# Alternating 128-slot and 64-slot experts in a mixture-of-experts stage, with some down weights multiplied unsplit in fp32

## The chip, the cores and the metric

The kernel runs on one core of a Trainium2 chip. The metric is the device time of one execution, in microseconds (us). Engines are written as the profile writes them: PE is TensorE (PEld its weight loads), DVE is VectorE, ACT is ScalarE, POOL is GpSimd, SP is the queue that issues the weight transfers.

## What is computed

A network of three blocks on 256 tokens of width 1024, all in fp32. The change touches the mixture-of-experts layer of the second block:

```python
def moe_swiglu(h, w_router, w_gate_up, w_down):
    t = h.reshape(-1, D)                       # 256 x 1024
    logits = (t @ w_router).astype(F32)
    top_val, top_idx = lax.top_k(logits, 2)    # 8 experts, 2 for each token
    top_w = jax.nn.softmax(top_val, axis=-1)
    ...
    for e in range(8):
        gt, up = jnp.split(t @ w_gate_up[e], 2, axis=-1)   # 1024 x 7168
        y = (jax.nn.silu(gt) * up) @ w_down[e]              # 3584 x 1024
        out = out + combine[:, e:e + 1] * y
```

## The kernel before

**Split products.** [...] To keep fp32 precision each fp32 operand is split into a high part H (ACT copies it to fp32r) and a low part L (DVE subtracts H from the raw value). A product is then H·H + H·L + L·H: three matmuls (`mm3`, L219 to L221). The weight split is `split` at L215: an ACTIVATE `wH<-raw` and a TENSOR_TENSOR `wL<-raw,wH` for each tile of 128x2048 (1 MiB).

**The weight stream.** `stream` (L149) hands out weight tiles in order: SP loads a raw tile (L161), ACT and DVE split it, and the tile is given to PE after `ahead` = 2 further tiles have been asked for. In this stage raw tiles have 10 buffers (`more_weights`: 4 of a pool "more", the 5 of "wraw", 1 spare), H has 3 and L has 3. An expert has 28 tiles of gate and up weights (W1) and 14 of down weights (W2, two for each 512-row chunk j = 0 to 6).

**Experts.** `route` sorts the experts by their number of tokens (expert 0 is put first always). Turns 0 to 3 get 128 slots each, turns 4 to 7 get 64 slots. `gather` picks the tokens of a group of turns with one-hot matmuls (`oh`) and writes them to the one pair of buffers `hH`, `hL`. For a big turn x is (H, L) of 128 slots and each weight slice of 512 columns takes 3 matmuls. For a small turn H and L of the 64 slots lie side by side as one stationary operand of 128 columns: `product` (L1197) makes one matmul x·wH of 128 columns (L1207) and one of the first 64 columns with wL (L1210), so 2 matmuls. The two halves of the result are added later: for the gate by a matmul with the fp32 matrix `fold` (L1251; operands `fold` and `halves` are plain fp32), for the activations by DVE (`both`, L1295), after which `both` is split into the two halves of `aH`.

**Order.** The loop goes over turns and over steps of 512-column chunks js = (0,), (1, 2), (3, 4), (5, 6). `up` does W1 of a step, then `down` does W2 of the step before; `finish` splits the result (`yH`, `yL`) and `scatter` adds it to the residual `xs` (L1383). Groups of turns gathered together are

```python
        groups = ((0,), (1, 2), (3,), (4, 5, 6, 7))
```

A gather stands ahead of the turn that begins a group, in the last step of the turn before. A branch for experts that overflow their slots stands behind the loop.

Of the kernel before, what the change touches and what calls it, by code (L numbers as in the profile page):

```python
# [10 lines left out]
F32 = mybir.dt.float32  # L11
# [20 lines left out]
BIG_TURNS = 4  # L32
# [54 lines left out]
class Net:  # L87
# [836 lines left out]
    def route(self, f, sb, psum):  # L924
# [9 lines left out]
        nc.gpsimd.tensor_copy(ones, self.cst["ones"])  # L934
        ident = self.cst["ident"]
# [77 lines left out]
        def order(counts):  # L1013
# [13 lines left out]
            turn = small("turn", [NE])  # L1027
            nc.vector.tensor_reduce(turn, a, axis=AX.X, op=OP.add)
            iota = self.cst["iota"][:, :NE]
            nc.vector.tensor_tensor(p, turn[:, None, :].to_broadcast(shape), iota[:, :, None].to_broadcast(shape),  # L1030
# [15 lines left out]
            nc.vector.tensor_scalar(full[:, BIG_TURNS:], full[:, BIG_TURNS:], 64.0, None, op0=OP.add)  # L1046
# [12 lines left out]
    def gather(self, sb, psum, route, turns, iota):  # L1059

        nc = self.nc
        n, small = len(turns), turns[0] >= BIG_TURNS
        w = 64 if small else 128
        place = route["place"][:, :, turns[0]:turns[0] + n]
        oh = sb.tile([128, 2, 4 if small else 2, 128], F32R, name="oh")[:, :, :n]
        for t in range(2):
            shape = [128, n, 128 // w, w]  # L1070
            nc.vector.tensor_tensor(oh[:, t].rearrange("p e (d s) -> p e d s", s=w),
                                    iota[:, None, None, :w].to_broadcast(shape),
                                    place[:, t, :, None, None].to_broadcast(shape), op=OP.is_equal)
        H, L = self.h_parts(other=False)
        g, hp = self.cols["moe_norm"], route["hp"]
        cols = n * w
        per = 512 // cols
        for c0 in range(0, KC, per):
            ps = psum.tile([128, 512], F32, name="tp", tag="tp")
            for k in range(c0, c0 + per):  # L1080
                o = ps[:, (k - c0) * cols:(k - c0 + 1) * cols].rearrange("p (e s) -> p e s", s=w)
# [3 lines left out]
                if small:  # L1085
                    for x, d in ((H, slice(0, 2)), (L, slice(2, 4))):
                        v = x[:, k].rearrange("p (e h s) -> p e h s", e=2, h=2)
                        nc.scalar.activation(v[:, :, 0], o[:, d], AF.Copy, scale=g[:, k:k + 1])
                        nc.vector.scalar_tensor_tensor(v[:, :, 1], o[:, d], g[:, k:k + 1], v[:, :, 0].bitcast(F32),
                                                       op0=OP.mult, op1=OP.subtract)  # L1090
                else:
                    o = ps[:, (k - c0) * cols:(k - c0 + 1) * cols]
                    nc.scalar.activation(H[:, k, :cols], o, AF.Copy, scale=g[:, k:k + 1])  # L1093
                    nc.vector.scalar_tensor_tensor(L[:, k, :cols], o, g[:, k:k + 1], H[:, k, :cols].bitcast(F32),
                                                   op0=OP.mult, op1=OP.subtract)
        x = []
        for i in range(n):
            s = slice(i % 2 * 128, i % 2 * 128 + 128)
            x.append(((H, L)[i // 2][:, :, s],) if small else (H[:, :, s], L[:, :, s]))

        def factors():
            rs = sb.tile([128, 4], F32, name="r_slot", bufs=2)
            ps = psum.tile([128, 512], F32, name="r_ps", tag="tp")
            for i in range(2 * n):
                nc.tensor.matmul(ps[:, i // 2 * 2:i // 2 * 2 + 2], oh[:, i % 2, i // 2], route["r"][:, i % 2],
                                 start=i % 2 == 0, stop=i % 2 == 1)
            nc.vector.tensor_reduce(rs[:, :n], ps[:, :2 * n].rearrange("p (e i) -> p e i", i=2), axis=AX.X, op=OP.add)
            return rs

        return x, oh, factors  # L1110

    def experts(self, sb, psum, route, iota_big, iota_small, ahead, x=None):
# [50 lines left out]
        def put_off(n, f):  # L1163
            later.append([n, f])
# [10 lines left out]
        def ohT(e):  # L1175

            if e not in ohTs:
                oh, i0 = by["oh"], e - by["e0"]
                n = min(2, by["n"] - i0)
                t_ = sb.tile([128, 2, T], F32R, name="ohT")  # L1180
                ps = psum.tile([128, 512], F32, name="tp", tag="tp")
                for i in range(2 * n):
                    self.transpose(ps[:, i * 128:(i + 1) * 128], oh[:, i % 2, i0 + i // 2].bitcast(F32))
                nc.scalar.copy(t_[:, :n].rearrange("p e t -> p (e t)"), ps[:, :n * T])
                for i in range(n):
                    ohTs[e + i] = t_[:, i]
            return ohTs[e]

        def fetch(group):
            e = group[0]  # L1190
            by["x"], by["oh"], by["factors"] = self.gather(sb, psum, route, group, iota_small if e >= BIG_TURNS else iota_big)
            by["e0"], by["n"] = e, len(group)
# [41 lines left out]
        def up(e, js):  # L1234

            small = e >= BIG_TURNS
            w = 64 if small else 128
# [4 lines left out]
            xe, i0 = by["x"][e - by["e0"]], e - by["e0"]  # L1242
# [17 lines left out]
            if js[0] == 0 and i0 == 0:  # L1260
                by["r"] = by["factors"]()
            r = by["r"][:, i0:i0 + 1]
            oh = by["oh"]
            acts = []

            def activations():
                for g in range(len(js)):
# [3 lines left out]
                    if gates:  # L1271
                        for i in range(4):
                            mm(gate, oh[:, i // 2, 0], gates[i // 2][i % 2].rearrange("p c s -> p (c s)"), start=i == 0, stop=i == 3)
# [7 lines left out]
            def parts(g):  # L1281
# [6 lines left out]
                with behind():  # L1288
                    if small:
# [11 lines left out]
                made.setdefault((e, js[g]), []).extend(y)  # L1301
# [3 lines left out]
        def down(e, j):  # L1305
# [491 lines left out]
```

## Time and profile before

| | us |
|---|---|
| median of 3 runs (1814.49 to 1816.99) | 1814.55 |
| the profiled execution, its device time | 1817.69 |
| its span in the trace | 1815.9 |
| PE busy / DVE busy / ACT busy in the span | 1706.0 / 1453.5 / 1208.2 |

Device time stands 1.8 us above the span in the profiled execution. A row of the windows lists, after the length, the busy time of PE, PEld, DVE, ACT and POOL with instruction counts, the granted TensorE clock as a share of full speed, and the share and rate of the DMA engines. The expert loop takes about half of the span; the profile's shares of busy time are means over stages with different limits, so the loop is read from its own windows.

### The profile page before, as it was taken

Reading aid. Unit: us, or ns where it says so; the run is one execution under the profiler, and the core shown is the slowest. Engines: PE = TensorE matmul, PEld = TensorE weight load, DVE = VectorE, ACT = ScalarE, POOL = GpSimd, SP = SyncE. Lnnn points to the kernel's source line nnn. Section 1 sums busy time; section 2 is a strip of 40 time slices with the busy share of each in tenths; the row PEclk is TensorE's granted clock in tenths of the full one; section 3 lists DMA queues with packets and bytes.
Section 4 is the critical chain, followed back from the end, with each engine's and each line's share of the span. In section 5 each row is a group of like instructions: output and inputs, shape, how many; then the busy total and the mean of one; then the engine's idle time right before and its main releaser. Section 6 shows DMA issues by size and latency. Waiting matters only on the chain. (4 is left out here: it accounts for less than half of the span.)

```text
span 1815.9 us, 21998 instructions
## 1 busy us (share of the span) xinstructions
PE 1706.0 (94%) x7875; PEld 1304.0 (72%) x7875; DVE 1453.5 (80%) x1545; ACT 1208.2 (67%) x1490; POOL 79.3 (4%) x116
## 2 busy tenths in 40 slices
PE   8999999999999999999999988888888869989997
PEld 6767787788778888888888755555555547778886
DVE  4767888666769988898898999999999966575555
ACT  6665444576557777777777888887888855654443
POOL 2102000020100000000000000000000010000001
PEclk9999999999999999999999999999999979999999
DMA  8537999553458999999999999999999934355551
GB/s 273 163 97 276 341 340 322 180 167 117 146 203 298 404 362 370 358 355 360 354 338 359 351 378 403 402 404 408 401 404 401 366 129 152 127 173 182 177 178 43
DMA packets 175894, 511.29 MB, mean 282 GB/s; under 512 B 10293, under 2 KB 36021, under 8 KB 172576
## 3 DMA queue, kind: packets, MB, share of 16 engines
q1 hardware_dynamic: 172720, 501.84, 75.4%
q0 software_dynamic: 2608, 7.11, 1.5%
q8 instruction: 64, 1.05, 0.2%
q10 hardware_dynamic: 448, 0.86, 0.1%
q14 instruction: 54, 0.44, 0.1%
HBM read 508.68 MB, written 2.66 MB: 282 GB/s over the span
## 5 line engine op out<-in xcount | busy, mean ns | idle before, releaser
L215 DVE TENSOR_TENSOR wL<-raw,wH 128x2048 fp32r<-128x2048 f32 (+2 forms) x665 | 1047.0, 1604 | 222.7 <-issue 87.9
L215 ACT ACTIVATE wH<-raw 128x2048 fp32r<-128x2048 f32 (+2 forms) x665 | 886.4, 1364 | 313.8 <-PE gu L221 120.1
L220 PE MATMUL gu<-wL,hH 128*128 128x512 f32 x744 | 292.6, 394 | 0.1
L221 PE MATMUL gu<-wH,hL 128*128 128x512 f32 x744 | 291.7, 393 | 0.0
L219 PE MATMUL gu<-wH,hH 128*128 128x512 f32 x744 | 286.5, 395 | 2.2 <-ACT hH L1093 2.2
L221 PE MATMUL acc<-wH,aL 128*128 128x512 f32 x440 | 174.7, 397 | 0.0
L220 PE MATMUL acc<-wL,aH 128*128 128x512 f32 x440 | 174.2, 396 | 0.3 <-DVE wL L215 0.3
L219 PE MATMUL acc<-wH,aH 128*128 128x512 f32 x440 | 172.5, 403 | 0.0
L220 PEld LDWEIGHTS gu<-wL,hH 128*128 128x128 f32 x744 | 141.0, 190 | 31.4 <-DVE wL L215 1.6
L219 PEld LDWEIGHTS gu<-wH,hH 128*128 128x128 f32 x744 | 140.8, 190 | 31.6 <-ACT hH L1093 2.3
L221 PEld LDWEIGHTS gu<-wH,hL 128*128 128x128 f32 x744 | 140.5, 189 | 29.3 <-DVE hL L1726 0.4
L219 PE MATMUL mm<-wH,hH 128*128 128x512 f32 (+1 forms) x384 | 152.0, 396 | 0.8 <-ACT hH L1725 0.5
L220 PE MATMUL mm<-wL,hH 128*128 128x512 f32 (+1 forms) x384 | 150.2, 392 | 0.0
L221 PE MATMUL mm<-wH,hL 128*128 128x512 f32 (+1 forms) x384 | 149.4, 390 | 0.0
L1210 PE MATMUL gu<-wL,hL 128*64 128x512 f32 x224 | 88.7, 413 | 20.0 <-DVE wL L215 19.5
L1210 PE MATMUL acc<-wL,aH 128*64 128x512 f32 x224 | 91.9, 417 | 16.0 <-DVE wL L215 11.9
L1210 PE MATMUL gu<-wL,hH 128*64 128x512 f32 x224 | 88.6, 413 | 17.4 <-DVE wL L215 16.9
L221 PEld LDWEIGHTS acc<-wH,aL 128*128 128x128 f32 x440 | 82.6, 188 | 19.6 <-issue 0.6
L220 PEld LDWEIGHTS acc<-wL,aH 128*128 128x128 f32 x440 | 82.7, 188 | 19.0 <-DVE wL L215 1.3
L219 PEld LDWEIGHTS acc<-wH,aH 128*128 128x128 f32 x440 | 82.5, 188 | 17.5
L1207 PE MATMUL acc<-wH,aH 128*128 128x512 f32 x224 | 89.3, 402 | 1.7 <-DVE aH L215 1.7
L1207 PE MATMUL gu<-wH,hH 128*128 128x512 f32 x224 | 85.6, 396 | 0.5 <-ACT wH L215 0.5
(480 smaller groups left out, 2100.0 us busy)
## 6 DMA issues: line engine op xcount, KB each, us to landing
raw<-in_moe_w_gate_up_dram SPq DMA_DIRECT2D x224, 1024.0 KB, 7.1
raw<-in_moe_w_down_dram SPq DMA_DIRECT2D x112, 1024.0 KB, 7.7
raw<-in_w_ff_dram SPq DMA_DIRECT2D x32, 1024.0 KB, 5.2
raw<-in_w_ada_dram SPq DMA_DIRECT2D x24, 1024.0 KB, 5.6
raw<-in_dense_w_gate_up_dram SPq DMA_DIRECT2D x44, 512.0 KB, 5.7
raw<-in_b_w_in_dram SPq DMA_DIRECT2D x12, 1024.0 KB, 5.2
raw<-in_w_in_dram SPq DMA_DIRECT2D x12, 1024.0 KB, 5.1
raw<-in_dense_w_down_dram SPq DMA_DIRECT2D x11, 1024.0 KB, 5.2
```

The lines of the kernel that those rows point to most:

```text
L215: return self.nc.scalar.activation(H, src, AF.Copy), self.nc.vector.tensor_tensor(L, src, H.bitcast(F32), op=OP.subtract)
L219: mm(ps, xH, wH, start=start, stop=False)
L220: mm(ps, xH, wL, start=False, stop=False)
L221: mm(ps, xL, wH, start=False, stop=stop)
L1207: high = lambda: mm(ps, x[0], H, start=start, stop=stop)
L1210: mm(ps[:64], x[0][:, :64], L, start=False, stop=False)
```

## The change

Three edits. (1) The rank of the expert at each turn comes from `RANKS`, so that turns 0, 2, 4, 6 are big (ranks 0 to 3) and 1, 3, 5, 7 small (ranks 4 to 7); the groups become (0), (1, 2), (3, 4), (5, 6), (7), each with at most one small and one big turn, gathered side by side in 256 columns. (2) For a small turn, the first of the two W2 tiles of each chunk j = 1 to 6 is not split (`whole`): PE multiplies the raw fp32 tile with the fp32 activations `both` (64 columns, `acc[h][:64]`), 4 products of 512 columns for a tile; `both` is then split only for the other half. (3) The pools of raw weights, "wraw" and "more", are allocated from the right end of SBUF.

```diff
-BIG_TURNS = 4
+RANKS = (0, 4, 1, 5, 2, 6, 3, 7)
...
-        with pool(name="wraw", bufs=raw) as a, pool(name="wh", bufs=high) as b, pool(name="wl", bufs=low) as c:
+        with pool(name="wraw", bufs=raw, side="right") as a, pool(name="wh", bufs=high) as b, pool(name="wl", bufs=low) as c:
...
-        with self.tc.tile_pool(name="more", bufs=more) as pool:
+        with self.tc.tile_pool(name="more", bufs=more, side="right") as pool:
...
-        for src in sources:
+        for src, parts in sources:
             raw = raw_(size)
             view = lambda x: x.rearrange("p (c b) -> p c b", b=src.shape[-1])
             nc.sync.dma_start(view(raw), src)
-            H = pH.tile([128, size], F32R, name="wH")
-            L = low_(size)
-            self.parts(H, L, raw)
-            made.append((view(H), view(L)))
+            if parts:
+                H = pH.tile([128, size], F32R, name="wH")
+                L = low_(size)
+                self.parts(H, L, raw)
+                made.append((view(H), view(L)))
+            else:
+                made.append((view(raw),))
...
-            nc.vector.tensor_scalar(full[:, BIG_TURNS:], full[:, BIG_TURNS:], 64.0, None, op0=OP.add)
+            nc.vector.tensor_scalar(full[:, 1::2], full[:, 1::2], 64.0, None, op0=OP.add)
...
+        d0, d1 = 0 if big is not None else 128, 192 if small is not None else 128
+        n = d1 - d0
+        per = 4 if n <= 128 else 2
...
+                o = ps[:, (k - c0) * n:(k - c0 + 1) * n]
                 for i in range(4):
-                    nc.tensor.matmul(o, hp[i // 2][:, i % 2, k * 128:(k + 1) * 128], oh[:, i % 2, :, :w],
+                    nc.tensor.matmul(o, hp[i // 2][:, i % 2, k * 128:(k + 1) * 128], one[:, i % 2, d0:d1],
                                      start=i == 0, stop=i == 3)
...
+                nc.scalar.activation(H[:, k, d0:d1], o, AF.Copy, scale=gk)
+                for e, d, w, to in ((big, 0, 128, L[:, k, :128]), (small, 128, 64, H[:, k, 192:])):
+                    if e is not None:
+                        nc.vector.scalar_tensor_tensor(to, o[:, d - d0:d - d0 + w], gk, H[:, k, d:d + w].bitcast(F32),
                                                        op0=OP.mult, op1=OP.subtract)
...
-        groups = ((0,), (1, 2), (3,), (4, 5, 6, 7))
+        groups = ((0,), (1, 2), (3, 4), (5, 6), (7,))
...
+        whole = lambda e, j, k0: e % 2 == 1 and j > 0 and k0 < 2
...
-                    yield W1[expert(e), :, k0:k0 + k, c0:c0 + n]
+                    yield W1[expert(e), :, k0:k0 + k, c0:c0 + n], True
...
-                        yield W2[expert(e), :, j, k0:k0 + k]
+                        yield W2[expert(e), :, j, k0:k0 + k], not whole(e, j, k0)
...
-            small = e >= BIG_TURNS
-            w = 64 if small else 128
+            small = e % 2 == 1
...
-                            put_off(0, lambda: split(y[0][:, :, :64], y[0][:, :, 64:], both))
+                            k = 2 if whole(e, js[g], 0) else 0
+                            put_off(0, lambda: split(y[0][:, k:, :64], y[0][:, k:, 64:], both[:, k:]))
...
-                H, L = take()
-                a = made[e, j]
+                w = take()
+                a, both = made[e, j]
                 for h in range(2):
                     d = slice(h * 512, (h + 1) * 512)
                     for k in range(k0, k0 + n):
-                        product(acc[h], [y[:, k] for y in a], H[:, k - k0, d], L[:, k - k0, d],
+                        if len(w) == 1:
+                            mm(acc[h][:64], both[:, k], w[0][:, k - k0, d], start=False, stop=False)
+                            continue
+                        product(acc[h], [y[:, k] for y in a], w[0][:, k - k0, d], w[1][:, k - k0, d],
                                 j == 0 and k == 0, j == steps[-1][-1] and k == 3)
```

The rest of the diff renames `turn` to `rank_`, makes the small tile `ranks` with eight memsets, and carries the one-hots and factors of a group by turn.

## Rows read from the trace of the kernel before

**Rows 1.** The page: span, and busy time of each engine.

```profile
span 1815.9 us, 21998 instructions
PE 1706.0 (94%) x7875; PEld 1304.0 (72%) x7875; DVE 1453.5 (80%) x1545; ACT 1208.2 (67%) x1490; POOL 79.3 (4%) x116
```

**Rows 2.** Timeline, ACT: first result split of expert 0, last split of the loop.

```profile
664.45 0.58 ACT L215 ACTIVATE yH<-acc 128x512 fp32r<-128x512 f32 x1
...
1467.85 0.58 ACT L215 ACTIVATE yH<-acc 128x512 fp32r<-128x512 f32 x1
```

**Rows 3.** Windows from `yH` to `yH`: length, busy, clock, DMA share, GB/s.

```profile
664.45:787.14 122.69, 122.69 (x552) 100.28 (x551) 108.41 (x65) 89.00 (x60) 0.00 (x0) 1.00 0.98 361
...
911.31:1037.59 126.28, 124.57 (x570) 99.66 (x569) 112.81 (x81) 93.14 (x77) 0.00 (x0) 1.00 0.95 348
...
1146.78:1255.76 108.98, 95.40 (x386) 58.96 (x386) 105.89 (x70) 90.67 (x74) 0.00 (x0) 1.00 1.03 403
...
1365.64:1467.85 102.21, 87.81 (x346) 54.74 (x346) 94.97 (x65) 80.80 (x69) 0.00 (x0) 0.97 0.88 341
sum 803.40, PE 746.64 PEld 534.70 DVE 744.93 ACT 626.48 POOL 0.00; mean PE 106.66 PEld 76.39 DVE 106.42 ACT 89.50 POOL 0.00
```

**Rows 4.** Waits, expert 4 (1146.78:1255.76): us in total, times, longest.

```profile
PEld gu L1210 <- DVE wL L215: 18.5, 21, 1.4
...
ACT wH L215 <- PE gu L1207: 8.7, 7, 2.9
```

**Rows 5.** Timeline, DVE, expert 4: start, us, instruction, count.

```profile
1164.55 8.89 DVE L215 TENSOR_TENSOR wL<-raw,wH 128x2048 fp32r<-128x2048 f32 x4
```

**Rows 6.** Timeline, PE, expert 5 (small): first and last of equal steps.

```profile
1276.63 0.40 PE L1207 MATMUL gu<-wH,hL 128*128 128x512 f32 x1
...
1278.24 0.62 PE L1207 MATMUL acc<-wH,aH 128*128 128x512 f32 x2
...
1281.04 0.40 PE L1207 MATMUL acc<-wH,aH 128*128 128x512 f32 x1
...
1282.67 0.62 PE L1207 MATMUL gu<-wH,hL 128*128 128x512 f32 x2
```

**Rows 7.** Timeline, PE, expert 3 (big): first and last of eight steps each.

```profile
959.78 0.39 PE L219 MATMUL gu<-wH,hH 128*128 128x512 f32 x1
...
961.60 0.62 PE L219 MATMUL gu<-wH,hH 128*128 128x512 f32 x2
...
965.02 0.39 PE L221 MATMUL acc<-wH,aL 128*128 128x512 f32 x1
...
966.89 0.39 PE L221 MATMUL acc<-wH,aL 128*128 128x512 f32 x1
```

**Rows 8.** Timeline, PE: two plain fp32 products (`fold`) among fp32r ones.

```profile
1268.70 1.88 PE L1251 MATMUL gu<-halves,fold 128*128 128x512 f32 x4
1270.02 0.79 PE L1210 MATMUL gu<-wL,hL 128*64 128x512 f32 x1
1270.65 0.39 PE L1207 MATMUL gu<-wH,hL 128*128 128x512 f32 x1
```

**Rows 9.** Groups of expert 4: weight loads of 64 columns, and transposes.

```profile
L1210 PEld LDWEIGHTS acc<-wL,aH 128*64 128x64 f32 x56 | 7.5, 134 | 11.2 <-DVE wL L215 9.3
...
L224 PE MATMUL tp<-cst,act 128*128 128x128 f32 x28 | 4.2, 272 | 0.0
```

**Rows 10.** Timeline, PE: first of eight gather matmuls, and the matmul after them.

```profile
1006.32 0.40 PE L1083 MATMUL tp<-oh,hpH 128*128 128x256 f32 x2
...
1007.26 0.40 PE L219 MATMUL acc<-wH,aH 128*128 128x512 f32 x1
```

**Rows 11.** A window of 4 us inside expert 4 (columns of rows 3).

```profile
1152.00:1156.00 4.00, 3.26 (x14) 2.07 (x14) 4.00 (x4) 2.87 (x2) 0.00 (x0) 1.00 1.03 411
```

**Rows 12.** DMA issues of expert 2 (787.14:911.31): count, KB, us to landing.

```profile
raw<-in_moe_w_gate_up_dram SPq DMA_DIRECT2D x29, 1024.0 KB, 7.0
```

**Rows 13.** Groups of expert 2: DVE's part of a gather for one big turn.

```profile
L1094 DVE SCALAR_TENSOR_TENSOR hL<-tp,c_moe_norm,hH 128x128 fp32r<-128x128 f32 x8 | 2.5, 345 | 0.4 <-ACT hH L1093 0.4
```

More of the change, by code (lines that the diff above doesn't have):

```diff
@@ L934, in route @@
         nc.gpsimd.tensor_copy(ones, self.cst["ones"])
+        ranks = sb.tile([128, NE], F32, name="ranks")
+        for i, x in enumerate(RANKS):
+            nc.gpsimd.memset(ranks[:, i:i + 1], float(x))
         ident = self.cst["ident"]
@@ L1026, in order @@
             nc.vector.tensor_tensor(a, a, b, op=OP.add)
-            turn = small("turn", [NE])
-            nc.vector.tensor_reduce(turn, a, axis=AX.X, op=OP.add)
+            rank_ = small("rank", [NE])
+            nc.vector.tensor_reduce(rank_, a, axis=AX.X, op=OP.add)
             iota = self.cst["iota"][:, :NE]
-            nc.vector.tensor_tensor(p, turn[:, None, :].to_broadcast(shape), iota[:, :, None].to_broadcast(shape),
+            nc.vector.tensor_tensor(p, rank_[:, None, :].to_broadcast(shape), ranks[:, :, None].to_broadcast(shape),
                                     op=OP.is_equal)
@@ L1057, in route, with gather @@
         return route
-    def gather(self, sb, psum, route, turns, iota):
+    def gather(self, sb, psum, route, turns, iota_big, iota_small):
         nc = self.nc
-        n, small = len(turns), turns[0] >= BIG_TURNS
-        w = 64 if small else 128
[L1067 to L1073, printed above, removed]
+        big, small = [next((e for e in turns if e % 2 == i), None) for i in range(2)]
+        one = sb.tile([128, 2, 256], F32R, name="oh")
+        for e, d, w, iota in ((big, 0, 128, iota_big), (small, 128, 64, iota_small)):
+            if e is None:
+                continue
+            place = route["place"][:, :, e:e + 1]
+            for t in range(2):
+                o = one[:, t, d:d + 128].rearrange("p (d s) -> p d s", s=w)
+                nc.vector.tensor_tensor(o, iota[:, None, :w].to_broadcast([128, 128 // w, w]),
+                                        place[:, t, :, None].to_broadcast([128, 128 // w, w]), op=OP.is_equal)
         H, L = self.h_parts(other=False)
         g, hp = self.cols["moe_norm"], route["hp"]
-        cols = n * w
-        per = 512 // cols
+        d0, d1 = 0 if big is not None else 128, 192 if small is not None else 128
+        n = d1 - d0
+        per = 4 if n <= 128 else 2
         for c0 in range(0, KC, per):
@@ L1080, in gather @@
             for k in range(c0, c0 + per):
-                o = ps[:, (k - c0) * cols:(k - c0 + 1) * cols].rearrange("p (e s) -> p e s", s=w)
+                o = ps[:, (k - c0) * n:(k - c0 + 1) * n]
                 for i in range(4):
-                    nc.tensor.matmul(o, hp[i // 2][:, i % 2, k * 128:(k + 1) * 128], oh[:, i % 2, :, :w],
+                    nc.tensor.matmul(o, hp[i // 2][:, i % 2, k * 128:(k + 1) * 128], one[:, i % 2, d0:d1],
                                      start=i == 0, stop=i == 3)
[L1085 to L1089, printed above, removed]
-                                                       op0=OP.mult, op1=OP.subtract)
[L1091 to L1099, printed above, removed]
+                gk = g[:, k:k + 1]
+                nc.scalar.activation(H[:, k, d0:d1], o, AF.Copy, scale=gk)
+                for e, d, w, to in ((big, 0, 128, L[:, k, :128]), (small, 128, 64, H[:, k, 192:])):
+                    if e is not None:
+                        nc.vector.scalar_tensor_tensor(to, o[:, d - d0:d - d0 + w], gk, H[:, k, d:d + w].bitcast(F32),
+                                                       op0=OP.mult, op1=OP.subtract)
@@ L1101, in factors @@
+        x, oh = {}, {}
+        if big is not None:
+            x[big], oh[big] = (H[:, :, :128], L[:, :, :128]), one[:, :, :128]
+        if small is not None:
+            x[small], oh[small] = (H[:, :, 128:],), one[:, :, 128:]
         def factors():
-            rs = sb.tile([128, 4], F32, name="r_slot", bufs=2)
+            rs = sb.tile([128, 2], F32, name="r_slot", bufs=2)
             ps = psum.tile([128, 512], F32, name="r_ps", tag="tp")
-            for i in range(2 * n):
-                nc.tensor.matmul(ps[:, i // 2 * 2:i // 2 * 2 + 2], oh[:, i % 2, i // 2], route["r"][:, i % 2],
-                                 start=i % 2 == 0, stop=i % 2 == 1)
@@ L1107, in factors @@
-            nc.vector.tensor_reduce(rs[:, :n], ps[:, :2 * n].rearrange("p (e i) -> p e i", i=2), axis=AX.X, op=OP.add)
-            return rs
+            for i, e in enumerate(turns):
+                for t in range(2):
+                    nc.tensor.matmul(ps[:, i * 2:i * 2 + 2], oh[e][:, t], route["r"][:, t], start=t == 0, stop=t == 1)
+            m = len(turns)
+            nc.vector.tensor_reduce(rs[:, :m], ps[:, :2 * m].rearrange("p (e i) -> p e i", i=2), axis=AX.X, op=OP.add)
+            return {e: rs[:, i:i + 1] for i, e in enumerate(turns)}
@@ L1177, in ohT @@
             if e not in ohTs:
-                oh, i0 = by["oh"], e - by["e0"]
-                n = min(2, by["n"] - i0)
                 t_ = sb.tile([128, 2, T], F32R, name="ohT")
                 ps = psum.tile([128, 512], F32, name="tp", tag="tp")
-                for i in range(2 * n):
-                    self.transpose(ps[:, i * 128:(i + 1) * 128], oh[:, i % 2, i0 + i // 2].bitcast(F32))
+                n = len(by["oh"])
+                for i, (turn, oh) in enumerate(by["oh"].items()):
+                    ohTs[turn] = t_[:, i]
+                    for t in range(2):
+                        self.transpose(ps[:, (i * 2 + t) * 128:(i * 2 + t + 1) * 128], oh[:, t].bitcast(F32))
                 nc.scalar.copy(t_[:, :n].rearrange("p e t -> p (e t)"), ps[:, :n * T])
-                for i in range(n):
-                    ohTs[e + i] = t_[:, i]
             return ohTs[e]
         def fetch(group):
-            e = group[0]
-            by["x"], by["oh"], by["factors"] = self.gather(sb, psum, route, group, iota_small if e >= BIG_TURNS else iota_big)
-            by["e0"], by["n"] = e, len(group)
+            by["x"], by["oh"], by["factors"] = self.gather(sb, psum, route, group, iota_big, iota_small)
         def w1(js):
@@ L1234, in up @@
         def up(e, js):
-            small = e >= BIG_TURNS
-            w = 64 if small else 128
+            small = e % 2 == 1
             gates = first_gates() if x is not None and e + js[0] == 0 else None
@@ L1241, in up @@
             gates = gates and gates()
[L1242 removed]
+            xe = by["x"][e]
             ps = [[psum.tile([128, 512], F32, name=f"gu{i}", tag="mm" if gates or i else "gu") for _ in js] for i in range(2)]
@@ L1259, in up @@
                     fold()
-            if js[0] == 0 and i0 == 0:
+            if js[0] == 0 and e in first:
                 by["r"] = by["factors"]()
-            r = by["r"][:, i0:i0 + 1]
-            oh = by["oh"]
+            r = by["r"][e]
+            oh = by["oh"][e]
             acts = []
@@ L1272, in activations @@
                         for i in range(4):
-                            mm(gate, oh[:, i // 2, 0], gates[i // 2][i % 2].rearrange("p c s -> p (c s)"), start=i == 0, stop=i == 3)
+                            mm(gate, oh[:, i // 2], gates[i // 2][i % 2].rearrange("p c s -> p (c s)"), start=i == 0, stop=i == 3)
                     with behind():
@@ L1300, in parts @@
                         self.split(*y, pt)
-                made.setdefault((e, js[g]), []).extend(y)
+                made[e, js[g]] = y, both if small else None
             return activations, parts
```

1 line of the change is left out of this document (added).

## Prediction

> **What bounds the kernel now.** I first took the page's span and busy shares [rows 1]. PE's 94% hides two regimes, so I cut the expert loop at each expert's first `yH` split, from 664.45 to 1467.85 us [rows 2], and read busy time, granted clock and transfer rate of each stretch [rows 3]. Before the first cut lies expert 0, which this change leaves almost alone; behind the last lie blocks that it does not touch. The reader should see that in a big expert's stretch PE is busy for all of it (122.69 of 122.69 us) at granted clock 1.00, with DVE at 108.41. In a small expert's stretch PE is busy 95.40 of 108.98 us and DVE 105.89. The waits of that stretch name the releaser: PE and its weight loads wait for `wL`, that is for DVE's half of the weight split [rows 4]. No transfer is among the long waits, though the rate there is 403 GB/s [rows 3]. So big experts are bound by PE, small ones by DVE, with the transfers close behind.
>
> **What DVE costs and what is taken off it.** Four back-to-back splits last 8.89 us with the tail of the last, so a split costs about 2.2 us of DVE [rows 5]. A small expert has 42 splits, 92.4 us, and the busy 105.89 less that leaves about 13.5 for all else, 1.9 for each of the seven chunks. Six tiles for each small expert lose their split: −13.2 us. Six of the seven `aH` splits are halved, worth under 0.2 us each, −1. DVE needs 105.9 − 14 = 92 us. ACT, at 90.67, loses six copies too and stays below.
>
> **What PE pays.** A small tile is 8 matmuls. Seven steps from 1276.63 to 1278.24 give 0.230 us each, 1.84 a W1 tile; seven from 1281.04 to 1282.67 give 0.233, 1.86 a W2 tile [rows 6]. A big tile is 12: eight steps in 1.82 and 1.87 us give 2.73 for W1 and 2.81 for W2 [rows 7]. The trace has no raw weight tile as a moving operand, but it has the same shape of plain fp32 product: `fold`, 512 columns, two records each. Four records start at 1268.70, one ordinary matmul follows, and the next starts at 1270.65. Less one ordinary step of 0.23 that is 1.72 us for two products, 0.86 each [rows 8]. A whole tile is 4 such products, 3.44 us instead of 1.86. Bounds: below, a product can't be cheaper than two fp32r steps, as it is two records (0.46, tile 1.86, no loss); above, add to each of its 8 records an unhidden 64-column weight load of 134 ns [rows 9], tile 4.51. I take 3.44, since the `fold` rows are the same operation and type.
>
> **Gathers.** Eight gather matmuls of 256 columns take 1007.26 − 1006.32 = 0.94 us, so 32 take 3.8 [rows 10]. There is one gather more than now; the three in the loop that hold a pair cost this each. The one for turn 7 alone has 64 columns and I charge it the same. The transposes of one expert's activations are 4.2 us, of its one-hots 0.6 (4 of them at 4.2/28) [rows 9].
>
> **The sum, PE alone.** Each stretch holds 24 W1 tiles of its own expert, 4 of the next, and 14 W2 tiles.
> Small, then big: 24 × 1.84 + 4 × 2.73 + 8 × 1.86 + 6 × 3.44 + 4.2 + 6 `fold` × 0.86 + 8 scatter matmuls × 0.234 = 44.2 + 10.9 + 14.9 + 20.6 + 4.2 + 5.2 + 1.9 = 101.9.
> Big, then small: 24 × 2.73 + 4 × 1.84 + 14 × 2.81 + 4.2 + 0.9 + 1.9 + 3.8 + 0.6 = 123.6.
> The last small one, with no next: 101.9 − 10.9 = 91.0.
> Three pairs and the last: 3 × 225.5 + 91.0 = 767.5, against 803.4 now [rows 3]. Expert 0's stretch now hands over to a small expert: 4 × (2.73 − 1.84) − 0.86 = 2.7 less. The floor's gain is 803.4 − 767.5 + 2.7 = 38.6 us.
>
> **What PE alone leaves out.** The big stretch that hands over to a small one today has the same sum, 123.6, and measures 126.28 [rows 3]: 2.7 us lost around the gather. The next expert's x goes to the one pair `hH`, `hL`, so its ACT and DVE copies start only after the last `up` matmul and queue behind splits; whoever starts the next `up` waits for them. I charge 2.7 to each of three big stretches, 8.1. DVE's gather work for a pair is two sets of eight instructions, at most 2 × 2.5 us by the one set of now [rows 13], and some one-hots; big stretches have 126.28 − 112.81 = 13 us of DVE idle to hide it, and without that cover the 5 would be paid three times. A small expert has PE at 102 and DVE at 92; but in its step (1, 2), where W2 is chunk 0 and split in full, DVE has 10 splits (22 us) and at most 2 × 1.9 for two chunks, against PE's 8 × 1.84 + 1.7 + 3.7 + 1.2 = 21.3. The lead of three split tiles, 6.6 us, covers the 4.5, nearly: I charge 1.0 for each of three, and 1.0 for the last one's tail; bounds 0 and 3.1, what DVE idles in a small stretch now (108.98 − 105.89). Total lost 12.1, so the gain is 38.6 − 12.1 = 26.5 us.
>
> **Edits at nothing.** The right-hand placement adds no instruction. Buffers that shared space with the stage before could be waited for earlier or later, but PE is not waiting for a weight transfer in the loop, so it hides under the ten buffers' lead. Rank memsets run on POOL, which is busy 79.3 us of the whole span [rows 1]. The raw buffer of a whole tile is now freed by PE and not by DVE, some three tiles later; SP's next issue into it waits, and behind it all later issues of the queue. Cover: in a big expert a tile lasts 122.69/42 = 2.9 us and lands after 7.0 [rows 3, 12], so 2.4 of ten buffers are in flight and about one in the split; six hold finished tiles.
>
> **Reference of the sum.** It is made in the profiled execution's span, 1815.9 [rows 1] (device time 1817.69); the median of the runs is 1814.55, 0.2% lower. I subtract the 26.5 from the median: 1788.
>
> **Rivals.**
> *Transfers become the bound in small experts.* The highest rate is 411 GB/s [rows 11], some 2.56 us a tile, so 42 tiles need 107.4 us and 38 (the last) 97.2. On average there is room: a pair takes 229 us on PE against 84 × 2.56 = 215. For it: within one small stretch of 103 us only 40.2 of 42 tiles arrive, and whole tiles hold buffers. Against it: the six finished tiles make up for those 1.8 and for two held buffers. If the lead were lost each time, the loop would take 3 × (107.4 + 126.3) + 97.2 = 798.3, a gain of 803.4 + 2.7 − 798.3 = 7.8: 1807. Chance 0.12.
> [...]
> *The fp32 products cost their weight loads too.* 24 tiles × 8 records × 134 ns [rows 9] = 25.7 us. Gain 0.8: 1814, no change. Against it: the four `fold` records run at 0.43 us each with 128-column loads under them [rows 8]. Chance 0.08.
> *Slower: DVE loses its lead.* `ahead` = 2 counts whole tiles, so in W2, where whole and split tiles take turns, fewer splits may be asked for ahead. If W1 then starts with no lead, a step costs DVE 8 × 2.2 + 3.8 = 21.4 by the time that PE has done 8 × 1.84 + 1.7 = 16.4: 5 lost in each of three steps of four experts, 60 us: 1788 + 60 = 1848. It decides from 26.5/12 = 2.2 us a step. Against it: splits are started by free buffers, and ACT already waits for PE to free a `wH` [rows 4]; whole tiles take none of those, so three buffers reach past them. Chance 0.10.
> *The forecast*, PE the bound in both kinds: 0.70, its own range 1770 to 1800 (no losses and transposes cheaper than charged at one end; twice the losses at the other).
>
> **How the numbers follow.** A measurement of this kernel tells changes from about 0.2% (3.6 us). Faster: forecast 0.70, transfers 0.12 and a quarter of the weight-load case, 0.02: 0.84. Same: the rest of that case, 0.06. Slower: 0.10. The range 1770 to 1812 holds the forecast, the transfer rival and some of the third, about 0.81.
>
> **What would show it.** In the profile after: small stretches near 103 us with PE busy nearly throughout and DVE near 92; 24 whole tiles with 3.4 us of PE each, records at 0.43; big stretches near 126; no wait of `wH` or `wL` for a transfer; 42 splits in a big stretch, 36 in a small one. Wrong, if PE's waits for `wL` stay in small experts, if raw transfers become a releaser, if the fp32 records stand more than 0.43 apart, or if each gather costs far more than 2.7.

## The result, and the profile after

The changed kernel takes 1833.41 us (median of 4 runs, 1832.71 to 1834.23) against 1814.74 for the kernel before: ratio 1.0099, 95% interval [1.0087, 1.0112]. It is 1.0% slower; the forecast was 1788, 1.5% faster, with 1812 as the upper end of the range.

The page of the changed kernel, as [rows 1]:

```profile
span 1830.7 us, 22036 instructions
PE 1742.1 (95%) x7907; PEld 1300.2 (71%) x7907; DVE 1402.7 (77%) x1554; ACT 1161.3 (63%) x1466; POOL 79.6 (4%) x124
```

DVE lost 51 us of work, as meant, and PE gained 36. Windows from `yH` to `yH`, columns as in [rows 3]; small, big, small stretch, then the last small one:

```profile
666.40:780.13 113.73, 108.58 (x411) 62.15 (x409) 93.17 (x65) 79.62 (x68) 0.00 (x0) 1.00 1.00 383
780.13:904.96 124.83, 122.12 (x557) 98.25 (x558) 111.73 (x82) 91.00 (x69) 0.00 (x0) 1.00 0.96 358
904.96:1019.43 114.47, 107.98 (x411) 62.62 (x409) 93.40 (x65) 79.41 (x67) 0.00 (x0) 1.00 0.99 380
...
1381.30:1483.06 101.76, 94.20 (x349) 51.80 (x348) 82.10 (x59) 68.63 (x63) 0.00 (x0) 1.00 0.84 319
sum 816.66, PE 784.50 PEld 534.62 DVE 694.05 ACT 579.14 POOL 0.00; mean PE 112.07 PEld 76.37 DVE 99.15 ACT 82.73 POOL 0.00
```

The loop has grown from 803.4 [rows 3] to 816.7 us. Big stretches are where the forecast had them or below (124.8 for 126.3). Small ones were to be 103 and 92 and are 114 and 102, though DVE is down to 93 as forecast and no transfer is among the waits. The waits of the stretch from 904.96 (us in total, times, longest), as [rows 4]:

```profile
ACT both L1294 <- PE tp L227: 15.6, 5, 5.1
DVE wL L218 <- ACT wH L218: 11.9, 9, 3.5
PEld acc L1322 <- issue: 11.4, 39, 0.4
PEld gu L1214 <- DVE wL L218: 10.6, 11, 1.3
```

So PE still waits for `wL`, from a DVE that is idle 21 us of the stretch: DVE waits for ACT's `wH`, and ACT stands at its copy `both`. The timelines of ACT, then DVE, around one block of down tiles (start, us, instruction, and in brackets the idle time before it with its releaser):

```profile
951.15 1.91 ACT L218 ACTIVATE wH<-raw 128x2048 fp32r<-128x2048 f32 x1
958.18 0.37 ACT L1294 COPY both<-tp 128x256 f32<-128x256 f32 x1 [5.12 <-PE tp L227]
958.45 1.91 ACT L218 ACTIVATE wH<-raw 128x2048 fp32r<-128x2048 f32 x1
962.35 0.38 ACT L1294 COPY both<-tp 128x256 f32<-128x256 f32 x1 [1.98 <-PE tp L227]
962.62 1.92 ACT L218 ACTIVATE wH<-raw 128x2048 fp32r<-128x2048 f32 x1
...
954.63 2.28 DVE L218 TENSOR_TENSOR wL<-raw,wH 128x2048 fp32r<-128x2048 f32 x1
960.39 2.29 DVE L218 TENSOR_TENSOR wL<-raw,wH 128x2048 fp32r<-128x2048 f32 x1 [3.48 <-ACT wH L218]
```

And PE's, through the end of the block and into the next step:

```profile
957.55 0.60 PE L227 MATMUL tp<-cst,act 128*128 128x128 f32 x4
958.08 3.65 PE L1322 MATMUL acc<-raw,both 128*64 128x512 f32 x8
961.65 0.65 PE L227 MATMUL tp<-cst,act 128*128 128x128 f32 x4
...
965.62 0.40 PE L1211 MATMUL gu<-wH,hH 128*128 128x512 f32 x1
966.91 0.45 PE L1214 MATMUL gu<-wL,hH 128*64 128x512 f32 x1 [0.90 <-DVE wL L218]
...
968.58 0.39 PE L1211 MATMUL gu<-wH,hH 128*128 128x512 f32 x1
969.65 0.45 PE L1214 MATMUL gu<-wL,hH 128*64 128x512 f32 x1 [0.68 <-DVE wL L218]
```

The reader is to see a ring: the transposes stand between whole tiles on PE; ACT's copy of their result stands ahead of the next `wH` copies; so in a block of some 12 us, where DVE was to build up its lead, it makes two splits (954.63 and 960.39); and the next step begins with late tiles, 1.29 us from one start to the next at 965.62, 1.07 at 968.58, instead of 0.23. Three late tiles stand behind this block and cost 2.4 us. In the trace ACT stands idle for 5.12 us ahead of one copy (958.18), and its next `wH` starts only behind that copy, at 958.45.

The ring is the smaller part. Ten matmuls of this stretch that wait for `wL` start 0.6 us or more behind the one ahead of them, where 0.23 is usual; they are 7.8 us late in all. Seven of them, 5.4 us, come before 943, ahead of the first whole tile at 949.95: whole tiles begin with chunk 1, so the step (1, 2) and the first eight W1 tiles of the next are split as before. The windows ahead of and behind that tile, in the changed kernel and then at the same place of alt_nowhole (the changed kernel without whole tiles, below):

```profile
904.96:949.95 44.99, 40.42 (x166) 25.57 (x164) 44.23 (x30) 36.96 (x31) 0.00 (x0) 1.00 1.01 387
949.95:1019.43 69.48, 67.56 (x247) 37.05 (x246) 49.17 (x36) 42.45 (x37) 0.00 (x0) 1.00 0.98 376
```

```profile
900.96:945.95 44.99, 40.28 (x165) 25.57 (x163) 44.37 (x30) 37.00 (x31) 0.00 (x0) 1.00 1.01 388
945.95:1011.08 65.13, 58.23 (x247) 38.66 (x246) 62.72 (x42) 54.09 (x43) 0.00 (x0) 1.00 1.03 405
```

Ahead of the whole tiles the two kernels are alike: DVE is busy for 44.2 of 45 us and sets the pace. Behind, DVE has 13.5 us less to do, but PE is busy 9.3 us longer, for 67.56 of 69.48 us, and that part takes 4.4 us more than when DVE set its pace. Nearly all of DVE's 21 idle us lie here, where they help nobody.

### The profile page after: what moved, and what is told of

Same layout as the page of the kernel before. It is cut to its first block, busy times and chain, and to the rows that moved or that the text cites. A ratio compares the mean times of both kernels' runs of the same rounds, so it can differ in the third digit from the quotient of the medians.

```text
span 1830.7 us, 22036 instructions
## 1 busy us (share of the span) xinstructions
PE 1742.1 (95%) x7907; PEld 1300.2 (71%) x7907; DVE 1402.7 (77%) x1554; ACT 1161.3 (63%) x1466; POOL 79.6 (4%) x124
## 5 line engine op out<-in xcount | busy, mean ns | idle before, releaser
L218 DVE TENSOR_TENSOR wL<-raw,wH 128x2048 fp32r<-128x2048 f32 (+2 forms) x641 | 992.8, 1579 | 255.2 <-ACT wH L218 97.2
L218 ACT ACTIVATE wH<-raw 128x2048 fp32r<-128x2048 f32 (+2 forms) x641 | 840.2, 1343 | 300.7 <-PE gu L224 109.4
L222 PE MATMUL gu<-wH,hH 128*128 128x512 f32 x744 | 280.2, 392 | 2.2 <-ACT hH L1094 2.2
L1214 PE MATMUL gu<-wL,hH 128*64 128x512 f32 x448 | 177.3, 413 | 23.6 <-DVE wL L218 23.1
L222 PE MATMUL acc<-wH,aH 128*128 128x512 f32 x440 | 173.5, 405 | 0.0
L1211 PE MATMUL gu<-wH,hH 128*128 128x512 f32 x448 | 169.8, 393 | 0.8 <-ACT act L1281 0.8
L222 PEld LDWEIGHTS gu<-wH,hH 128*128 128x128 f32 x744 | 139.8, 188 | 31.4 <-ACT hH L1094 2.3
L1211 PEld LDWEIGHTS gu<-wH,hH 128*128 128x128 f32 x448 | 84.1, 188 | 38.4 <-issue 3.2
L1214 PEld LDWEIGHTS gu<-wL,hH 128*64 128x64 f32 x448 | 59.7, 134 | 72.7 <-DVE wL L218 42.2
L1322 PE MATMUL acc<-raw,both 128*64 128x512 f32 x192 | 90.1, 602 | 0.0
```

The costliest lines, as they stand in the source:

```text
L218: return self.nc.scalar.activation(H, src, AF.Copy), self.nc.vector.tensor_tensor(L, src, H.bitcast(F32), op=OP.subtract)
L222: mm(ps, xH, wH, start=start, stop=False)
L1211: high = lambda: mm(ps, x[0], H, start=start, stop=stop)
L1214: mm(ps[:64], x[0][:, :64], L, start=False, stop=False)
L1322: mm(acc[h][:64], both[:, k], w[0][:, k - k0, d], start=False, stop=False)
```

## The experiments

Each kernel was timed in 3 rounds beside the kernel before on the same chip (the last two in 5); the medians of the kernel before lie between 1814.74 and 1817.21 us on the chips used, so kernels are compared by their ratios and by their windows. The theory at the start: ACT's copy in front of the weight copies. Rivals: what the narrow fp32 weight loads cost, alternation, placement, the lead.

**Whole tiles off (alt_nowhole), whole tiles alone (whole_old), placement alone (right_only).**

```diff
# alt_nowhole, from the changed kernel
-        whole = lambda e, j, k0: e % 2 == 1 and j > 0 and k0 < 2
+        whole = lambda e, j, k0: False
# whole_old, from the kernel before: `whole`, `parts` of the stream and the branch in `down`, as in the change
+        whole = lambda e, j, k0: e >= BIG_TURNS and j > 0 and k0 < 2
# right_only, from the kernel before: side="right" in "wraw" and "more"
```

> The changed kernel with every down tile split again: alternation and right-hand placement alone. If the loss sits in the whole fp32 tiles (theory: ACT's copy `both` stands in front of the next weight copies and waits for transposes that now lie behind whole tiles), the small stretches are bound by DVE again at about 109 us with 42 splits, the big ones stay near 124, and the time is 1811 to 1819 us. If alternation and the wider gathers carry the loss, it stays at 1826 or above.

> The kernel before (small experts together at the end, left-hand placement) with only the whole fp32 tiles. If whole tiles alone jam the splits, small stretches stand near 114 us and the last near 102, as in the changed kernel, so the time is about 803.4 + 3 x 5 = 15 us above the kernel before: 1825 to 1832. If the jam needs a big expert on either side, small stretches fall to about 103 and the time to 1795 to 1803.

> The kernel before with only the right-hand placement of the raw weight pools. Both theories: no change, 1813 to 1817 us. If placement carries part of the loss (later first transfers of a stage, or contention), 2 us or more above the kernel before.

Measured: alt_nowhole 1817.46 us, ratio 1.0016 [1.0004, 1.0028]; whole_old 1826.73, 1.0063 [1.0047, 1.0080]; right_only 1815.53, 0.9994 [0.9985, 1.0004]. Placement costs nothing. Alternation alone costs about 0.2%, though its loop is shorter (800.7 us for 803.4). Of that difference 2.7 us are the last stretch of the kernel before, 102.21 us at a granted clock of 0.97 [rows 3]; in right_only the same stretch took 99.56 at 1.00 and the loop 800.8. So the loops are alike, and the handover from expert 0, below, shows where the cost may lie. Whole tiles alone cost 0.6%, so they carry the loss; their small stretches are 111.6 to 113.4 us, the last 100.8. The parts do not add up to 0.99%; why the two together cost more was not separated.

**The narrow loads (wide).**

```diff
-                        both = sb.tile([128, 4, 64], F32, name="both", tag="aL", bufs=2)
-                        nc.scalar.copy(both, pt[:, :, 64:])
+                        both = sb.tile([128, 4, 128], F32, name="both", tag="aL", bufs=2)
+                        nc.scalar.copy(both, pt)
...
-                            mm(acc[h][:64], both[:, k], w[0][:, k - k0, d], start=False, stop=False)
+                            mm(acc[h], both[:, k], w[0][:, k - k0, d], start=False, stop=False)
```

> The changed kernel with a whole tile's product made with 128 stationary columns: `both` holds the two halves side by side and the halves are added with those of the split tiles at the end. Theory of the copy in front of ACT's queue: that order stays, so at most 4 us are won (1829 to 1834). Rival, the 64-column fp32 weight loads that are not pulled ahead at each entry and exit of a whole group, about 9 groups x 0.29 us in a small stretch: about 10 us are won, 1822 to 1825.

Measured: 1825.14 us, 1.0048 [1.0031, 1.0064]. A group of four whole records and the matmuls around it on PE, in the changed kernel and then in wide:

```profile
949.63 0.39 PE L1211 MATMUL gu<-wH,hH 128*128 128x512 f32 x1
949.95 1.93 PE L1322 MATMUL acc<-raw,both 128*64 128x512 f32 x4
951.81 0.45 PE L1214 MATMUL gu<-wL,hH 128*64 128x512 f32 x1
952.09 0.40 PE L1211 MATMUL gu<-wH,hH 128*128 128x512 f32 x1
```

```profile
953.57 0.39 PE L1211 MATMUL gu<-wH,hH 128*128 128x512 f32 x1
953.80 1.88 PE L1322 MATMUL acc<-raw,both 128*128 128x512 f32 x4
955.12 0.80 PE L1214 MATMUL gu<-wL,hH 128*64 128x512 f32 x1
955.75 0.40 PE L1211 MATMUL gu<-wH,hH 128*128 128x512 f32 x1
```

The weight load of the first record, narrow and then wide:

```profile
949.94 0.19 PEld L1322 LDWEIGHTS acc<-raw,both 128*64 128x64 f32 x2 [0.36 <-issue]
```

```profile
953.57 0.42 PEld L1322 LDWEIGHTS acc<-raw,both 128*128 128x128 f32 x2
```

The narrow load starts with its matmul (949.95), the wide one 0.23 us ahead of it (953.80). From the L1211 ahead to the L1211 behind: 2.46 us narrow, 2.18 wide. So each group costs 0.28 us more, nine groups 2.5 a stretch; the stretch fell from 114.47 to 112.13. This rival holds, as a second cause of the smaller size.

**The queue and the lead, one at a time (copy_late, parts_early, second, ahead_split, spread, deep, raw8).** Each from the changed kernel:

```diff
# copy_late
-                        nc.scalar.copy(both, pt[:, :, 64:])
+                        def copy():
+                            with behind():
+                                nc.scalar.copy(both, pt[:, :, 64:])
+                            put_off(0, add)
...
-                        put_off(0, add)
+                        put_off(0, copy)
# parts_early
-                                put_off(ahead - 1 + g, lambda g=g, parts=parts: parts(g))
+                                put_off(ahead - 2 + g, lambda g=g, parts=parts: parts(g))
# second
-        whole = lambda e, j, k0: e % 2 == 1 and j > 0 and k0 < 2
+        whole = lambda e, j, k0: e % 2 == 1 and j < 6 and k0 >= 2
# ahead_split
-            if len(made) > ahead:
+            while sum(len(m) == 2 for m in made) > ahead:
                 yield made.pop(0)
# spread: sources() and the loop take the tiles of a step in this order (1: a down tile of a small expert)
+            k = min(n // 2, m)
+            return [0] * (n - k) + [1, 0] * k + [1] * (m - k)
# raw8
-            with self.more_weights(RAW, 4, 2):
+            with self.more_weights(RAW, 2, 2):
# deep: as raw8, and a fourth wH and a fourth wL of pools of their own
+            highs = itertools.cycle([high_] * 3 + [lambda n: mh.tile([128, n], F32R, name="wH")])
```

> The changed kernel with ACT's copy `both` put off by one tile, so that it is issued behind the next weight copy wH. Theory of the copy in ACT's queue: ACT's waits for transposes (15.6 us in a small stretch) fall by half and PE's waits for wL with them, small stretches to about 109, the time to 1812 to 1822 us; if PE waits for `both` in its place, nothing is won. Rival, fp32 weight loads and lead: unchanged, 1831 to 1836.

> The changed kernel with each set of transposes put one tile earlier, in big and in small experts. Theory of the copy in ACT's queue: the transposes come ahead of the whole tile that holds them up, ACT's longest wait for them falls from 5.1 to about 3 us, the time by 8 to 15, to 1818 to 1825. Rivals: unchanged within 3 us.

> The changed kernel with the second tile of each chunk j = 0 to 5 whole in place of the first of each chunk j = 1 to 6: as many whole tiles, but the two that stood next to each other around a chunk's end no longer do, and `both` is wanted one tile later. Theory of the copy in ACT's queue: less PE work lies between a copy's issue and its transposes, small stretches fall to about 109, the time to 1812 to 1822. Rival that each entry and exit of a whole group costs 0.29 us: 12 groups in place of 9, 3 to 4 us more, about 1837.

> The changed kernel, but a tile is handed to TensorE when two further split tiles have been asked for; whole tiles no longer count as lead. Rival (the way the prediction told it: the lead is counted in tiles, and whole ones give DVE none): PE's waits for wL in small stretches go and these fall from 114 to about 105, the time to 1795 to 1805 us. Theory of the copy `both` in ACT's queue: the splits that are asked for earlier still stand behind that copy, small stretches stay above 111, the time above 1822.

> The changed kernel with the down tiles of a small expert not in a block behind the eight gate and up tiles of the next step, but one by one between the last of those. Theory of the lead (eight split tiles in a row cost DVE 21.4 us where PE has done them in 16.4, and three buffers bring too little of a lead out of the block of whole tiles): the block is gone, PE's waits for wL in a small stretch fall from 16 to under 6 us, small stretches to 104 to 106, the time to 1797 to 1808 us. Rival, only the entries and exits of whole groups and the copy in ACT's queue count: more groups, so 1830 or more.

> The changed kernel with one more buffer for wH and one for wL in the expert loop, in the place of two raw ones (eight raw). Theory of the lead: one more tile, 2.2 us, is carried into each of three steps of a small expert, so small stretches fall by 4 to 6.6 us and the time to 1808 to 1818 us. Rival, ACT's queue stands behind a copy whatever the buffers: at most 3 us better. The price of two raw buffers less is seen in raw8.

> The changed kernel with eight raw buffers in place of ten, nothing else. If the raw buffers that wait for whole tiles on PE starve the transfers (rival), small stretches grow by 3 us or more each and the time passes 1845. Theories of the lead and of ACT's queue: 1832 to 1838.

| kernel | us | ratio to before [95%] | loop, us |
|---|---|---|---|
| changed | 1833.41 | 1.0099 [1.0087, 1.0112] | 816.7 |
| copy_late | 1829.05 | 1.0066 [1.0046, 1.0086] | 810.7 |
| parts_early | 1834.40 | 1.0091 [1.0071, 1.0111] | 813.8 |
| second | 1835.59 | 1.0091 [1.0066, 1.0116] | 815.3 |
| ahead_split | 1843.56 | 1.0148 [1.0127, 1.0169] | 824.0 |
| spread | 1838.86 | 1.0131 [1.0108, 1.0153] | 819.4 |
| deep | 1829.00 | 1.0079 [1.0055, 1.0103] | 815.0 |
| raw8 | 1833.37 | 1.0099 [1.0079, 1.0120] | 816.6 |

None brought the gain that a theory asked of it; parts_early, ahead_split, spread and raw8 came out where no gain was expected. ahead_split speaks against the reason that the prediction gave for its slower rival (the count in `ahead`): asked for earlier, the splits came no sooner for PE (17.4 us of waits for `wL` in the stretch from 906, 16.4 before), and its loss lies in the last stretch, 108.65 us for 101.76. raw8 excludes the raw buffers. spread cut PE's waits for `wL` but brought waits for `halves` and `act` and no gain. copy_late took ACT's longest wait for `tp` from 5.1 to 2.4 us, as meant, and won only 1.3 us in the stretch from 904; in its place ACT waits 8.9 us (6.7 before it) for PE to free a `wH`. In deep that buffer is there, and ACT's wait for `tp` grows from 15.6 to 20.9 us. So the theory of the queue alone fell. Read together, the two suggest that queue and buffers bound the lead in turn.

**Both together (late_deep, late_wide_deep, old_late_wide_deep), and the control (late_before_deep).** late_deep is copy_late and deep in one; late_wide_deep adds wide; old_late_wide_deep has all three on whole_old; late_before_deep has copy_late and deep on the kernel before.

> The changed kernel with the copy put off by one tile (copy_late) and one more buffer each for wH and wL, eight raw (deep). Theory that both bound the lead in turn (with three buffers the fourth weight copy can't start, with the copy ahead of it it may not): only together do they let DVE run on through the block of whole tiles, PE's waits for wL at the start of a step (about 8 us in a small stretch) fall to 2 to 3, small stretches to 108 or 109, the time to 1805 to 1815. If the two only add up (1.3 + 0.5 us a stretch): 1824 to 1827, and the lead is set by something else.

> As late_deep, with the product of 128 stationary columns. Theory that both bound the lead in turn, and 2.3 us a stretch for the narrow loads: small stretches 105 to 107, 1796 to 1807 us, faster than the kernel before. If the parts only add up: 1816 to 1819.

> The kernel before (small experts last, left-hand placement) with whole tiles in 128 stationary columns, the copy put off and the fourth buffers. Theory that the lead was all that was lost: small stretches 101 to 104 (no big expert's tiles at their end), 1790 to 1803 us. If the parts only add up on whole_old: about 1811 to 1815.

> The kernel before, without whole tiles, with the copy put off and the fourth buffers: the control. DVE is busy 106 of 109 us in a small stretch there, so neither can give more than 3 us a stretch: 1805 to 1816 us, with 1812 to 1816 the likeliest.

Measured: late_deep 1815.99 us, 0.9998 [0.9988, 1.0007]; late_wide_deep 1805.43, 0.9940 [0.9923, 0.9956]; old_late_wide_deep 1804.79, 0.9934 [0.9917, 0.9951]; late_before_deep 1808.21, 0.9948 [0.9932, 0.9965]. The loop lost 6.0 us by copy_late and 1.7 by deep, but 16 by both. Small stretches of late_deep, windows as above:

```profile
895.21:1006.09 110.88, 107.81 (x412) 63.28 (x410) 91.81 (x66) 78.97 (x67) 0.00 (x0) 1.00 1.00 387
...
1364.15:1461.40 97.25, 93.97 (x350) 52.57 (x349) 80.54 (x58) 71.06 (x67) 0.00 (x0) 1.00 0.98 376
```

That the two act together is shown: no late tile is left behind the first whole one, and PE waits for `wL` four times in the stretch, 2.7 us in all, where it does so ten times and 6.3 us in the changed kernel. The size was over-estimated (110.9 us, not 108 to 109), since the late tiles ahead of it only fell from 5.4 to 3.2 us. late_wide_deep came into its range, with stretches longer than expected (108.3 us, not 105 to 107), old_late_wide_deep 2 us above its range. The control tells more: without any whole tile the same two edits win 0.5%. Three of its small stretches are 3.9, 3.5 and 1.8 us shorter, about the 3 us each that I had thought to be left at most. The lead was short in the kernel before, too.

In old_late_wide_deep three small stretches follow each other, and the third is bound by transfers. Its window, and the waits in it:

```profile
1247.52:1358.00 110.48, 102.75 (x394) 62.01 (x393) 92.60 (x63) 82.21 (x69) 0.00 (x0) 1.00 1.03 407
```

```profile
ACT wH L220 <- DMA raw<-in_moe_w_down_dram: 16.2, 8, 3.5
...
ACT wH L220 <- DMA raw<-in_moe_w_gate_up_dram: 8.9, 18, 1.8
```

The two before it are 105.5 and 105.3 us. Alternation (late_wide_deep) keeps clear of this, with 391 GB/s and 6.6 us of such waits in the stretch from 893, but its loop is no shorter, 791.7 us in both kernels.

**Spread and wide (spread_wide).**

> Spread and the product of 128 stationary columns together. Theory of the lead and the 64-column loads both: the parts add up, small stretches near 102, 1788 to 1798 us. If spread gives nothing, as wide alone, about 1825.

Measured: 1821.65 us, 1.0032 [1.0020, 1.0045]. The wide form wins 17 us on spread, more than the 8 on the changed kernel; 0.28 us a group does not explain that, and the cause stays open; with it its small stretches are 110 us, still bound by the waits named above.

**How many whole tiles (half_whole, alt_late_deep).**

```diff
# half_whole, from late_wide_deep
-        whole = lambda e, j, k0: e % 2 == 1 and j > 0 and k0 < 2
+        whole = lambda e, j, k0: e % 2 == 1 and j % 2 == 1 and k0 < 2
# alt_late_deep, from late_deep
+        whole = lambda e, j, k0: False
```

> late_wide_deep with three whole tiles for each small expert (chunks 1, 3 and 5) in place of six. A whole tile costs PE 1.6 us more than a split one and saves DVE 2.2. Theory that PE's own work is now the larger part of a small stretch (late_wide_deep: 108.3 us with DVE busy 91): PE falls by 4.7, DVE rises to 98, small stretches to 105 or 106 and the time to 1795 to 1802 us. Rival, DVE's order within a step is still what counts: small stretches as before or longer, 1805 to 1810.

> late_deep without any whole tile: what the whole tiles bring once the lead is there. If the whole tiles pay by then (late_deep 1816, late_wide_deep 1805): 1808 to 1814 us, DVE busy 106 in small stretches of 107 to 109. If the lead and the copy alone were the gain, it is at or below late_wide_deep: 1800 to 1806.

Measured: half_whole 1797.45 us, 0.9897 [0.9882, 0.9913]; alt_late_deep 1802.11, 0.9919 [0.9906, 0.9933]. One small stretch and the last one, of half_whole and then of alt_late_deep:

```profile
892.36:998.17 105.81, 100.74 (x412) 66.30 (x410) 98.28 (x69) 86.11 (x70) 0.00 (x0) 1.00 1.01 392
...
1350.74:1444.74 94.00, 87.87 (x352) 55.46 (x351) 86.50 (x61) 76.03 (x66) 0.00 (x0) 1.00 0.99 379
```

```profile
891.22:997.43 106.21, 98.51 (x412) 64.74 (x410) 104.86 (x72) 89.89 (x72) 0.00 (x0) 1.00 1.02 394
...
1350.33:1450.28 99.95, 88.29 (x352) 55.88 (x351) 93.62 (x64) 80.88 (x71) 0.00 (x0) 0.97 0.99 380
```

With the lead in place, six narrow whole tiles cost 14 us (late_deep against alt_late_deep), six wide ones 3, and three wide ones win 5 (0.8%, 0.2% and 0.2% by the ratios; at 0.2% the intervals overlap). By the windows three wide ones win 0.4 us in each of the first three small stretches, and 6.0 in the last, where the clock of alt_late_deep was 0.97; six wide ones lose 2 in each of the three and win 3.8 in the last. Whether their number or the choice of chunks 1, 3 and 5 matters was not separated. half_whole is the fastest, 1.0% below the kernel before.

## Why the prediction was wrong, by its own steps

**Right.** DVE's work (92 us forecast, 93.4 measured), the fp32 records at 0.43 us (eight records with a switch ahead of them, 3.57 us from 958.08 to 961.65), the big stretches, the raw buffers at nothing (raw8), placement at nothing (right_only).

**The step that failed** is the loss of a small stretch: "The lead of three split tiles, 6.6 us, covers the 4.5, nearly: I charge 1.0". The sum of PE's work, 101.9, holds to about 2 us; the stretch took 114.47. Of the 12.6 between, 5.4 are the late tiles ahead of the first whole one, where 1.0 was charged, 2.4 those behind the first block, 2.5 the nine narrow groups, and some 2 are spread over many steps. The argument took the lead for given, looked at the step (1, 2) alone, though the next eight W1 tiles are split without relief too, and its bound of 3.1 (what DVE idled before) was no bound: it spoke of a kernel in which DVE was the limit throughout. With whole tiles DVE is the limit up to the first of them and PE behind it, and what counts is how much work passes from one part to the other. Three buffers and ACT's queue limited that in turn; both mended together gave back 3.6 of the 12.6 (late_deep). The four small stretches are 43.7 us longer than forecast (444.4 for 400.7), the big ones 6.6 shorter. The whole miss is 45: 37.1 in the loop, 4.7 ahead of it (expert 0, below), and some 3 in the reference, as the profiled execution of the kernel before stood 3.1 us above the median from which the gain was subtracted.

**The slower rival** had the sign, and about the place (W1 short of a lead, 7.8 us lost over three steps where it took 15), at a chance of 0.10. But two of the three steps come before any whole tile of their expert, and its reason, the count in `ahead`, is not borne out by ahead_split. The argument against it, that three buffers reach past the whole tiles, overlooked what else stands in ACT's queue; the copy `both` was not in the working at all.

**The rival of the fp32 weight loads** was priced by record (134 ns) and is paid by group: 0.28 us at its ends and little between, as loads inside a group stand 0.43 us apart in both widths (950.43 and 950.86 narrow, 954.23 and 954.66 in wide). In the two groups shown above the first load started 0.23 us ahead of its matmul with 128 columns of fp32 (wide), and 0.01 us ahead with 64. **Transfers** were not the bound in the changed kernel, where no wait of the stretch from 904.96 is for one; they were where the lead was mended and small experts follow each other (25 us of ACT's waits in old_late_wide_deep).

**Expert 0** was to end 2.7 us earlier by the tiles it hands over to. It did not: the loop's first `yH` came at 666.40 us for 664.45 [rows 2], though such starts differ by 4.6 us between programs that are alike up to there (669.00 in right_only), so only the windows inside it count. PE around 630 us, before and then after:

```profile
630.00:640.00 10.00, 10.00 (x57) 8.51 (x56) 9.41 (x13) 7.83 (x10) 0.00 (x0) 1.00 1.03 408
```

```profile
620.00:630.00 10.00, 8.08 (x42) 6.27 (x40) 9.38 (x13) 6.47 (x9) 0.00 (x0) 1.00 1.04 400
630.00:640.00 10.00, 9.41 (x35) 7.65 (x36) 5.44 (x14) 4.02 (x6) 0.00 (x0) 0.66 0.74 292
```

Matmuls of the gather for turns 1 and 2 in the changed kernel:

```profile
628.82 0.44 PE L1091 MATMUL tp<-oh,hpH 128*128 128x192 f32 x2 [1.47 <-DVE hH L1097]
...
631.04 0.44 PE L1091 MATMUL tp<-oh,hpH 128*128 128x192 f32 x2 [0.45 <-ACT hH L1094]
...
631.77 0.71 PE L1091 MATMUL tp<-oh,hpH 128*128 128x192 f32 x2
```

The gather runs almost alone on PE and waits for its ACT and DVE copies between its matmuls (8.08 us busy of the ten from 620). From about 632 to 638 the granted clock is 0.50, with the matmuls of 512 columns in it 0.43 us apart (635.51 to 638.07); the mean from 630 to 640 is 0.66. alt_nowhole shows the same 0.66, so whole tiles are not the cause. But late_deep, late_wide_deep and alt_late_deep, alternated too, show 1.00 there, though PE waits in the same gather (it is busy for 8.23 of those ten us in late_deep), and half_whole 0.83. So the waits of PE belong to alternation; what decides whether the clock falls stays open.

## What to carry to other kernels

Where work is moved between two engines that take turns as the limit, compare them for each part of the work, not for a whole stretch, and see in which part the relief falls: here it fell where PE had the most to do, and left the part that DVE bounds as it was. Follow also how much finished work can pass between the parts: buffers, and every instruction in the queue that makes it. Two limits in series hide each other, so that mending either alone seems worthless. And once the lead is there, move less: here half of the whole tiles gained a little where all of them lost.

## What was not expected of the hardware

In the changed kernel the first plain fp32 matmul of a group, with 64 stationary columns, started its weight load only with its own turn (949.94 and 949.95): 0.28 us a group more than with 128 columns in wide (2.46 and 2.18). Loads ran at 407 GB/s over a whole small expert of old_late_wide_deep, and ACT waited 25 us for them in it. In the changed kernel the granted clock fell to half some 6 us into a gather whose matmuls were broken by waits of 0.45 to 1.47 us; the later gathers of the same kernel show 1.00 in their stretches, and so does the same gather in late_deep.
